# Hybrid encoder block on one core: full-row score and decay matmuls, and a quarter of the bias row copies

## The chip, the cores and the metric

The kernel runs on one core of a Trainium2 chip. The metric is the device time of one execution in microseconds, taken as the median of several runs.

## What is computed

One layer of a bidirectional encoder: 1024 tokens of width 1024. The normalised input goes through one projection whose columns serve two groups of heads: eight attention heads (two key heads, width 64) that see 128 tokens to either side, and four gated delta-rule heads (width 128) that run over the tokens in both directions. Their outputs pass `w_out`, and a feed-forward layer with a squared relu of width 4096 follows. The parts that matter here:

```
scores = einsum(q, k_band) * 64**-0.5 + bias[head, query, key - query]   # band: previous, own, next block of 128
scores = where(valid, scores, -1e30);  probs = softmax([scores, sink])
...
gc     = cumsum(g)                                     # per chunk, head, direction
decay  = exp(where(causal, gc[..., :, None] - gc[..., None, :], -inf))
a_mat  = where(strict, beta * (k @ k.T) * decay, 0);   t_mat = inverse(I + a_mat)
```

## The kernel before, in words

All large products are made in float32r with the operands split into a high and a low part: three matmuls of 128x512 for each 128 rows of the contraction (L118 to L122, `mm3`). Four engines work beside TensorE (PE): VectorE (DVE), ScalarE (ACT), GpSimd (POOL), and SyncE (SP), which issues nearly all the DMAs. PSUM is used as two rings of four banks, `psA` and `psB`; SBUF tiles come from rings too (`pg` with 28, `pt` with 12, `wr` with 4 buffers), so that a tile's buffer comes free when its last reader is done, a DMA included.

The program is written as Python generators that emit instructions, and `weave` (L51) runs two of them side by side by weights. A scheduler then sets the order on each engine once, at build time; each engine works through its own list in order. `phases` (L1026) has these stages:

- The input is normalised, transposed and split, and the a, b, k and q columns are projected. `gates` (L298) makes the cumulative decays `gc` by token and transposes them into rows; they are kept in three bfloat16 parts, two on the 128 rows of `g12`, the third on the 64 rows of `g3`.
- `bias_rows` (L500) makes the bias by relative position for 8 heads (8 x 512) with one matmul and writes it to DRAM, `biasd`, in 128 copies, one for each query row, so that reading with a pitch of 511 gives a band shifted by one per row.
- Projections of v, z and the attention's k, v, q are woven with `prep` (L615). For each of 8 chunks of 128 tokens and 2 directions, `prep` broadcasts a row of `gc` over all partitions for each of 4 heads: a matmul of a one-hot column (`selb`) against `g12` (L630), one of 64 rows against `g3` (L632), and one that adds the mask (L634). ScalarE takes the exponential (L637), VectorE multiplies by the Gram products (L641, L649), ScalarE copies the diagonal 32x32 blocks out (L646), and SP stores the results (`atd`, `pd`). Then `eliminate` (L653) inverts these blocks by 31 steps of elimination on VectorE for each direction (L669, L671; transposes L658, L680, L681), and `invert` (L685) builds the full inverses with small matmuls on PE (from L714).
- `proj_attn` (L457) keeps the attention keys' high part of each key head on both partition halves (`kh`, two tiles), and the low parts of both heads in one tile (`kl`), 64 rows each. Queries go to DRAM (`qad`, L493) and come back with the high part on 64 partitions and the low part on the other 64. `bias_table` (L514) loads the band of each pair of heads from `biasd` (L520).
- `attention` (L588) is woven with the first scan of the delta rule (`scan`, L762). For each block, key head and query head one matmul of 128 rows (L536: query high and low against key high) and one of 64 rows (L537: query high against key low) accumulate into a bank; VectorE adds the bias and takes the maximum (L538); exponentials on ScalarE (L550), scaling (L555), transposes on PE (L565), values (L576).
- The second scan runs beside the output projections, and then comes the feed-forward layer.

Of the kernel before, what the change touches and what calls it, by code (L numbers as in the profile page):

```python
# [9 lines left out]
F32 = mybir.dt.float32  # L10
# [23 lines left out]
def bucket_onehot():  # L34
    """Rows of the Toeplitz bias by relative position: 32 bucket selectors and the window mask."""
# [38 lines left out]
class Block:  # L74
# [30 lines left out]
    def small(self, shape, bufs=12, tag="sm"):  # L105
        return self.buf(tag, bufs, shape)
# [5 lines left out]
    def split(self, raw, h, l):  # L112
        """raw = h + l exactly, both float32r."""
# [34 lines left out]
    def setup2(self):  # L148
# [18 lines left out]
        self.selb = t("selb", (P, 64), BF16)  # L167
        nc.gpsimd.tensor_tensor(out=self.selb, in0=self.ident[:, 0:64], in1=self.ident[:, 64:128], op=ALU.add)
# [44 lines left out]
    def transpose_split(self, rows, w, pstag, out):  # L213
        """rows: 4 tiles [tok, D] -> per k a tile [d, (high, low), 512 tokens], scaled by w[:, k]."""
# [7 lines left out]
    def transpose_first(self, rows, w, out):  # L222
        """The same, row by row as the rows arrive, through all banks."""
# [8 lines left out]
    def load_w(self, srcs):  # L232
        """srcs(k half) -> list of (column slice, dram AP [p, 4, cols])."""
# [23 lines left out]
    def pair(self, raws, order=None):  # L257
        """The two column tiles of a load: (tile, half, psum), both tiles of one half first."""
# [39 lines left out]
    def gates(self, ps):  # L298
        """Per token: gc, its exponentials, beta. Layout [tok, chunk, dir * 4 + head]."""
# [35 lines left out]
        gc2 = self.small((P, 2, NT, 8), bufs=1, tag="gc2")  # L335
        self.ngc, self.egc, self.negc, self.egl, self.ew = (mk(n) for n in ("ngc", "egc", "negc", "egl", "ew"))
        for r in range(2):
            vt.tensor_copy(out=gc2[:, r], in_=gps[:, 0])
        vt.tensor_scalar(out=self.ngc, in0=gc2[:, 0], scalar1=-1.0, scalar2=None, op0=ALU.mult)
        nc.scalar.activation(out=self.egc, in_=gc2[:, 0], func=AF.Exp)  # L340
        vt.tensor_scalar(out=self.negc, in0=self.egc, scalar1=-1.0, scalar2=None, op0=ALU.mult)
        nc.scalar.activation(out=self.egl, in_=gps[:, 1], func=AF.Exp)
        vt.tensor_tensor(out=self.ew, in0=gps[:, 1], in1=gc2[:, 0], op=ALU.subtract)
        nc.scalar.activation(out=self.ew, in_=self.ew, func=AF.Exp)
        # gc by rows, in three bfloat16 parts
        tp = self.ps("psB", (P, P))
        nc.tensor.transpose(tp, gc2.rearrange("p r c x -> p (r c x)"), self.ident)
        self.g12 = c.tile([P, P], BF16, name="g12")
        self.g3 = c.tile([64, P], BF16, name="g3")
        rr = self.sc((P, 4, P))  # L350
        r1, b1 = rr[:, 0, :], rr[:, 1, :]
        nc.scalar.copy(out=self.g12, in_=tp)
        vt.tensor_copy(out=b1, in_=self.g12)
        vt.tensor_tensor(out=r1, in0=tp, in1=b1, op=ALU.subtract)
        vt.tensor_copy(out=self.g12[64:128, :], in_=r1[64:128, :])
        b2b = rr[0:64, 2, :]
        b2h = c.tile([64, P], BF16, name="b2h")
        vt.tensor_copy(out=b2h, in_=r1[0:64, :])
        vt.tensor_copy(out=b2b, in_=b2h)
        vt.tensor_tensor(out=self.g3, in0=r1[0:64, :], in1=b2b, op=ALU.subtract)  # L360
        self.cc, self.w2 = mk("cc"), mk("w2")

    def conv_silu(self, ct, raw, out):
        """Five taps along tokens, then silu."""
# [10 lines left out]
    def proj_conv(self, c0, kind, raws=None):  # L375
        """k, v or q columns of the delta rule heads, two heads a load."""
# [80 lines left out]
    def proj_attn(self):  # L457
        """Keys: the high part of each kv head on both partition halves, the low parts of both. Values: by tokens.
        Queries: scaled, to DRAM."""
# [4 lines left out]
        self.kh, self.kl = [self.pg(dt=F32R) for _ in range(2)], self.pg(dt=F32R)  # L464
        self.va = self.pg((P, NT, P))
        for i, half, ps in self.pair(raws):
# [3 lines left out]
            if i == 0:  # L470
# [3 lines left out]
                for v, (r, o) in enumerate(((lo, up), (up, lo))):  # L474
                    nc.scalar.copy(out=self.kh[v][r, tok], in_=t[r, :])
                    nc.scalar.copy(out=self.kh[v][o, tok], in_=swap[o, :])
                    nc.gpsimd.tensor_tensor(out=self.kl[r, tok], in0=t[r, :], in1=self.kh[v][r, tok].bitcast(F32),
# [22 lines left out]
    def bias_rows(self):  # L500
        """rel_bias by relative position, a copy per query row, so that rows of pitch 511 read it as a band."""
# [10 lines left out]
        nc.sync.dma_start(out=self.biasd, in_=row.unsqueeze(1).to_broadcast([8, P, 512]))  # L512

    def bias_table(self):  # L514
        self.bias = []
        for b in range(4):
            t = self.pg((P, 2, 3 * P))
            src = bass.AP(tensor=self.biasd.tensor, offset=self.biasd.offset + 2 * b * P * 512 + P - 1,
                          ap=[[511, P], [P * 512, 2], [1, 3 * P]])
            self.nc.sync.dma_start(out=t, in_=src)  # L520
            self.bias.append(t)

    def attn_scores(self, n, kv, mx, q, mk):
# [3 lines left out]
        rows = slice(64 * kv, 64 * kv + 64)  # L527
        tiles = []
        for gp in range(2):
            s = mk((P, 2, 3 * P))  # L530
            for i in range(2):
# [5 lines left out]
                nc.tensor.matmul(ps[:, :width], q[rows, g, :], self.kl[rows, keys], start=False, stop=True)  # L537
# [44 lines left out]
    def query(self, n, kv):  # L582
        """Queries' high parts on the partitions of their keys, the low parts on the others."""
# [4 lines left out]
    def attention(self):  # L588
        """Scores run ahead of the transposes of the probabilities by two steps of one block and key head."""
# [528 lines left out]
```

## Time and profile before

| | us |
|---|---|
| median of 3 runs (lowest, highest) | 1373.59 (1372.97, 1377.02) |
| span of the profiled execution | 1372.6 |
| PE busy in the span | 1335.4 |
| VectorE busy in the span | 661.1 |
| ScalarE busy in the span | 471.4 |
| windowed attention beside the first scan (358 to 515) | 157 |

The profile is of one execution. A row of a timeline gives the start, the length, the engine, the line in the kernel, the operation, and the tiles written and read. A matmul's length includes its way through the array, so that neighbours overlap: what a matmul costs in a row of others is read from start to start. Two engines can each be busy for most of a stage, and the stage ends with the one whose list ends last.

### The profile page before, as it was taken

The page shows a single profiled execution, that of the slowest core. Times are in us where ns is not written, and L with a number is a line of the kernel's source. Part 1 is how long each engine was busy: PE and PEld are TensorE (multiplying, and loading weights), DVE is VectorE, ACT ScalarE, POOL GpSimd, SP SyncE. Part 2 cuts the span into 40 slices and gives each one's busy share as a digit, 9 for nine tenths or more (in the row PEclk, how much of TensorE's full clock was granted, in tenths as well). Part 3 has the DMA queues.
Part 4 walks back from the last instruction along what each step waited for, and adds up shares of the span by engine and source line. Part 5 has one row for each costly group of instructions (what it writes and reads, how often), then busy time and mean ns, then how long its engine had stood idle before and what let it go on. Part 6 is the DMA issues. An engine that isn't in the chain of part 4 may idle for free.

```text
span 1372.6 us, 18620 instructions
## 1 busy us (share of the span) xinstructions
PE 1335.4 (97%) x7026; PEld 1056.2 (77%) x7026; DVE 661.1 (48%) x1339; ACT 471.4 (34%) x1085; POOL 463.3 (34%) x429
## 2 busy tenths in 40 slices
PE   7999969989999999999999999999999999999997
PEld 5788757868766668888888888888888888888885
DVE  4676636982467877575332233223332233223336
ACT  6464747445545553124412212122112211221113
POOL 4353200362422224143414332333323331433123
PEclk9999989999789999999999999999999999999999
DMA  6142463433835548121111110121011101121003
GB/s 218 62 135 97 65 196 124 146 116 80 214 108 147 161 153 305 64 62 62 62 32 62 62 47 16 62 62 62 16 46 62 62 31 32 62 62 57 20 1 123
DMA packets 86186, 121.97 MB, mean 89 GB/s; under 512 B 6627, under 2 KB 59952, under 8 KB 86097
## 3 DMA queue, kind: packets, MB, share of 16 engines
q1 hardware_dynamic: 77396, 116.30, 26.8%
q0 software_dynamic: 8448, 4.20, 1.6%
q8 instruction: 55, 0.90, 0.3%
q10 hardware_dynamic: 253, 0.30, 0.1%
q14 instruction: 34, 0.28, 0.1%
HBM read 88.79 MB, written 31.46 MB: 88 GB/s over the span
## 4 chain that ended last, share of the span: by engine, by line
PE 88%; DVE 6%; DMA 4%; issue 1%; ACT 1%; POOL 0%; POOLq 0%; DVEq 0%; ACTq 0%
PE psA L120 15%; PE psA L122 15%; PE psA L121 15%; PE psB L121 9%; PE psB L120 9%; PE psB L122 9%; PE psB L791 4%; DMA biasd<-pt 3%; PE psA L576 2%; PE psA L537 2%; PE psA L565 2%; DVE pt L669 2%; PE psA L536 2%; DVE sc L671 1%; DVE pg L671 1%
## 5 line engine op out<-in xcount | busy, mean ns | idle before, releaser
L122 PE MATMUL psA<-pg,wl 128*128 128x512 f32 x864 | 342.1, 397 | 0.8 <-POOL wl L116 0.8
L121 PE MATMUL psA<-pg,wh 128*128 128x512 f32 x864 | 342.3, 397 | 0.0
L120 PE MATMUL psA<-pg,wh 128*128 128x512 f32 x864 | 342.1, 397 | 0.2 <-ACT pg L208 0.2
L982 DVE TENSOR_TENSOR pg<-pg,psB 128x512 f32<-128x512 f32 x256 | 175.7, 688 | 277.1 <-PE psB L122 275.7
L116 POOL TENSOR_TENSOR wl<-wr,wh 128x512 fp32r<-128x512 f32 x108 | 156.3, 1469 | 291.6 <-ACT wh L115 291.5
L121 PE MATMUL psB<-sc,pg 128*128 128x512 f32 x512 | 202.5, 396 | 0.0
L120 PE MATMUL psB<-sc,pg 128*128 128x512 f32 x512 | 201.2, 394 | 0.0
L122 PE MATMUL psB<-sc,pg 128*128 128x512 f32 x512 | 200.8, 392 | 0.0
L122 PEld LDWEIGHTS psA<-pg,wl 128*128 128x128 f32 x864 | 163.0, 189 | 38.6 <-POOL wl L116 1.2
L121 PEld LDWEIGHTS psA<-pg,wh 128*128 128x128 f32 x864 | 163.0, 189 | 38.3 <-issue 0.9
L120 PEld LDWEIGHTS psA<-pg,wh 128*128 128x128 f32 x864 | 163.0, 189 | 37.8 <-ACT pg L208 0.6
L116 POOL TENSOR_TENSOR sc<-wr,sc 128x512 fp32r<-128x512 f32 x64 | 81.7, 1299 | 174.9 <-ACT sc L115 174.9
L964 DVE SCALAR_TENSOR_TENSOR pt<-psA,pt 128x512 f32<-128x512 f32 x64 | 44.1, 690 | 197.6 <-ACT pt L963 197.6
L966 POOL TENSOR_TENSOR pg<-pt,pg 128x512 fp32r<-128x512 f32 x64 | 82.2, 1294 | 157.4 <-ACT pg L965 157.4
L115 ACT CAST wh<-wr 128x512 fp32r<-128x512 f32 x108 | 61.7, 620 | 167.8 <-PE psA L121 144.4
L120 PEld LDWEIGHTS psB<-sc,pg 128*128 128x128 f32 x512 | 96.1, 188 | 23.9 <-ACT sc L115 0.6
L121 PEld LDWEIGHTS psB<-sc,pg 128*128 128x128 f32 x512 | 96.2, 188 | 22.6 <-POOL sc L116 0.5
L122 PEld LDWEIGHTS psB<-sc,pg 128*128 128x128 f32 x512 | 96.0, 188 | 22.3
L115 ACT CAST sc<-wr 128x512 fp32r<-128x512 f32 x64 | 36.4, 618 | 185.1 <-PE psB L121 185.1
L965 ACT CAST pg<-pt 128x512 fp32r<-128x512 f32 x64 | 39.6, 618 | 147.4 <-issue 122.3
L963 ACT ACTIVATE pt<-psA 128x512 f32<-128x512 f32 x64 | 37.8, 593 | 81.1 <-PE psA L122 81.1
L791 PE MATMUL psB<-sc,pg 128*128 128x128 f32 x320 | 47.8, 281 | 2.2 <-DVE pg L830 1.4
(288 smaller groups left out, 1774.2 us busy)
## 6 DMA issues: line engine op xcount, KB each, us to landing
wr<-in_w_ffn_in SPq DMA_DIRECT2D x32, 512.0 KB, 4.6
wr<-in_w_ffn_out SPq DMA_DIRECT2D x32, 512.0 KB, 3.6
wr<-in_w_in SPq DMA_DIRECT2D x22, 512.0 KB, 5.8
pg<-in_x SPq DMA_DIRECT2D x16, 512.0 KB, 5.2
sc<-kvd SPq DMA_DIRECT2D x14, 512.0 KB, 4.0
kvd<-pt SPq DMA_DIRECT2D x16, 256.0 KB, 4.4
atd<-pt SPq DMA_DIRECT2D x16, 256.0 KB, 5.0
pd<-pt SPq DMA_DIRECT2D x16, 256.0 KB, 3.3
```

What stands on the lines that cost most here:

```text
L115: nc.scalar.copy(out=h, in_=raw)
L116: nc.gpsimd.tensor_tensor(out=l, in0=raw, in1=h.bitcast(F32), op=ALU.subtract)
L120: nc.tensor.matmul(ps, wh, xh, start=first, stop=False)
L121: nc.tensor.matmul(ps, wh, xl, start=False, stop=False)
L122: nc.tensor.matmul(ps, wl, xh, start=False, stop=last)
L536: nc.tensor.matmul(ps[:, :width], q[:, g, :], self.kh[kv][:, keys], start=True, stop=False)
L791: nc.tensor.matmul(ps[:, h - g.start, :], left(h), right[:, h, :], start=True, stop=True)
L963: nc.scalar.activation(out=r, in_=ps, func=AF.Relu)
L964: nc.vector.scalar_tensor_tensor(out=q, in0=ps, scalar=0.0, in1=r, op0=ALU.max, op1=ALU.mult)
L965: nc.scalar.copy(out=a[:, 0], in_=q)
L966: nc.gpsimd.tensor_tensor(out=a[:, 1], in0=q, in1=a[:, 0].bitcast(F32), op=ALU.subtract)
L982: nc.vector.tensor_tensor(out=self.h[t][:, sl], in0=self.h[t][:, sl], in1=ps, op=ALU.add)
```

## The change

- `prep`: the three parts of the decay rows are laid on rows 0 to 47 of one tile `grow` (row 16 r + 2 chunk + direction for part r, the four heads side by side on the free axis), with zeros on the other rows. `selb` has ones at i, i + 16 and i + 32. One matmul of 128 rows and 512 columns makes the rows of all four heads, and one of 512 columns adds the mask.
- `gates`: one copy of `gc` where there were two; the parts are made on 64 rows, written to DRAM (`gcd`, three DMAs), and read back as `grow` (one DMA).
- `proj_attn` and `attn_scores`: a tile of low key parts for each key head, with zeros on the 64 rows that held the other head, so that the second score matmul has 128 rows as well. VectorE writes the zeros.
- `bias_rows` and `bias_table`: 32 copies of each bias row, not 128; the table of two heads is loaded by four DMAs of 32 partitions, each from another offset.

The diff, cut to its core:

```diff
-        self.selb = t("selb", (P, 64), BF16)
-        nc.gpsimd.tensor_tensor(out=self.selb, in0=self.ident[:, 0:64], in1=self.ident[:, 64:128], op=ALU.add)
+        self.selb, self.zero = t("selb", (P, 16), BF16), t("zero", (P, 1))
+        nc.gpsimd.memset(self.zero, 0.0)
+        nc.gpsimd.tensor_tensor(out=self.selb, in0=self.ident[:, 0:16], in1=self.ident[:, 16:32], op=ALU.add)
+        nc.gpsimd.tensor_tensor(out=self.selb, in0=self.selb, in1=self.ident[:, 32:48], op=ALU.add)
...
+        self.grow = c.tile([P, GH, P], BF16, name="grow")
+        nc.gpsimd.memset(self.grow, 0.0)
+        for r in range(3):
+            nc.sync.dma_start(out=self.gcd[r], in_=part[:, r, :])
+        nc.sync.dma_start(out=self.grow[0:48], in_=self.gcd.rearrange("r (a h) t -> (r a) h t", h=GH))
...
-        self.kh, self.kl = [self.pg(dt=F32R) for _ in range(2)], self.pg(dt=F32R)
+        self.kh, self.kl = [self.pg(dt=F32R) for _ in range(2)], [self.pg(dt=F32R) for _ in range(2)]
+        for v, o in enumerate((up, lo)):
+            nc.vector.tensor_copy(out=self.kl[v][o, :], in_=self.zero[o, :].to_broadcast([64, SEQ]))
...
-        nc.sync.dma_start(out=self.biasd, in_=row.unsqueeze(1).to_broadcast([8, P, 512]))
+        nc.sync.dma_start(out=self.biasd, in_=row.unsqueeze(1).to_broadcast([8, 32, 512]))
...
-            src = bass.AP(tensor=self.biasd.tensor, offset=self.biasd.offset + 2 * b * P * 512 + P - 1,
-                          ap=[[511, P], [P * 512, 2], [1, 3 * P]])
-            self.nc.sync.dma_start(out=t, in_=src)
+            for m in range(4):
+                src = bass.AP(tensor=self.biasd.tensor,
+                              offset=self.biasd.offset + 2 * b * 32 * 512 + P - 1 - 32 * m,
+                              ap=[[511, 32], [32 * 512, 2], [1, 3 * P]])
+                self.nc.sync.dma_start(out=t[32 * m:32 * m + 32], in_=src)
...
-                nc.tensor.matmul(ps[:, :width], q[rows, g, :], self.kl[rows, keys], start=False, stop=True)
+                nc.tensor.matmul(ps[:, :width], q[:, g, :], self.kl[kv][:, keys], start=False, stop=True)
...
-                for h in range(GH):
-                    i = 8 * c + 4 * d + h
-                    nc.tensor.matmul(rows[:, h, :], self.selb[:, i:i + 1].to_broadcast([P, P]), self.g12,
-                                     start=True, stop=False)
-                    nc.tensor.matmul(rows[:, h, :], self.selb[0:64, i:i + 1].to_broadcast([64, P]), self.g3,
-                                     start=False, stop=False)
-                    nc.tensor.matmul(rows[:, h, :], self.identb, self.maskb[d], start=False, stop=True)
+                i = 2 * c + d
+                nc.tensor.matmul(rows, self.selb[:, i:i + 1].to_broadcast([P, P]), self.grow, start=True, stop=False)
+                nc.tensor.matmul(rows, self.identb, self.maskb[d].unsqueeze(1).to_broadcast([P, GH, P]),
+                                 start=False, stop=True)
```

The scheduler sets the order anew, and it differs at many places by a few rows. Three of them follow; line numbers after the change are those of the changed file, which runs two to three lines ahead at these places.

PE's list at the first chunk's decay rows, before (`g_507` is `g12`, `g_508` is `g3`, and the three matmuls with their loads follow for each head):

```order
L630 LDWEIGHTS selb
L630 MATMUL psB_1292<-g_507,selb 128x128
L632 LDWEIGHTS selb
L632 MATMUL psB_1292<-g_508,selb 128x128
L634 LDWEIGHTS identb
L634 MATMUL psB_1292<-maskb_127,identb 128x128
```

The same place after the change, with the first matmul of the chunk's second direction behind it (`psB_1318`):

```order
L633 LDWEIGHTS selb
L633 MATMUL psB_1298<-grow,selb 128x512
L634 LDWEIGHTS identb
L634 MATMUL psB_1298<-maskb_128,identb 128x512
L633 LDWEIGHTS selb
L633 MATMUL psB_1318<-grow,selb 128x512
```

What stood there were 12 matmuls for each direction, and now there are 2. The projection matmuls among which they stand moved too: ahead of the last decay row of all there are 664 `mm3` matmuls in PE's list, where there were 636; ahead of the first matmul of the inversion 870, where there were 879; ahead of the first score 1056 in both.

VectorE's list near the end of the elimination, before (`pg` tiles are of the first direction, `sc` tiles of the second, L469 empties a bank of the key projection):

```order
L671 TENSOR_TENSOR pg_2075<-pg_2075,pt_2078 128x31
L669 TENSOR_TENSOR pt_2388<-sc_2383,sc_2385 128x220
L680 STREAM_TRANSPOSE pg_2342<-pg_2075 128x1024
L681 STREAM_TRANSPOSE pg_2341<-pg_2075 128x1024
L671 TENSOR_TENSOR sc_2385<-sc_2385,pt_2388 128x10x22
L469 COPY pt_2616<-psA_2591 128x512
```

The same place after the change:

```order
L672 TENSOR_TENSOR pg_1921<-pg_1921,pt_1924 128x31
L672 TENSOR_TENSOR sc_2231<-sc_2231,pt_2234 128x6x26
L681 STREAM_TRANSPOSE pg_2188<-pg_1921 128x1024
L682 STREAM_TRANSPOSE pg_2187<-pg_1921 128x1024
L467 CAST pg_2375<-zero 64x1024
L467 CAST pg_2376<-zero 64x1024
L670 TENSOR_TENSOR pt_2234<-sc_2229,sc_2231 128x135
L484 COPY pg_2379<-psB_2467 128x512
```

The two fills of zeros stand between the end of the first direction's elimination and the end of the second's.

SP's list at the bias table, before (`atd` loads feed the inversion, `qad` stores are the queries):

```order
L493 DMA qad<-pt_3044 64x512 x2
L520 DMA pg_3315<-biasd 128x2x384
L520 DMA pg_3317<-biasd 128x2x384
L520 DMA pg_3319<-biasd 128x2x384
L520 DMA pg_3321<-biasd 128x2x384
L701 DMA pg_3360<-atd 128x2x512
L701 DMA pg_3364<-atd 128x2x512
```

The same place after the change:

```order
L496 DMA qad<-pt_2893 64x512 x2
L525 DMA pg_3164<-biasd 32x2x384 x4
L525 DMA pg_3169<-biasd 32x2x384 x4
L525 DMA pg_3174<-biasd 32x2x384 x4
L525 DMA pg_3179<-biasd 32x2x384 x2
L496 DMA qad<-pt_2968 64x512 x2
```

Sixteen loads stand where four stood; the last two of them, and the two `atd` loads of a later step, come behind further query stores.

More of the change, by code (lines that the diff above doesn't have):

```diff
@@ L103, in pt, with small @@
         return self.buf("pt", 12, shape, dt)
-    def small(self, shape, bufs=12, tag="sm"):
-        return self.buf(tag, bufs, shape)
+    def small(self, shape, bufs=12, tag="sm", dt=F32):
+        return self.buf(tag, bufs, shape, dt)
     def ps(self, tag, shape=(P, HALF)):
@@ L334, in gates @@
         nc.tensor.matmul(gps[:, 1], self.ones, g, start=True, stop=True)
-        gc2 = self.small((P, 2, NT, 8), bufs=1, tag="gc2")
+        gc2 = self.small((P, NT, 8), bufs=1, tag="gc2")
         self.ngc, self.egc, self.negc, self.egl, self.ew = (mk(n) for n in ("ngc", "egc", "negc", "egl", "ew"))
[L337 to L340, printed above, removed]
+        vt.tensor_copy(out=gc2, in_=gps[:, 0])
@@ L341, in gates @@
+        vt.tensor_scalar(out=self.ngc, in0=gc2, scalar1=-1.0, scalar2=None, op0=ALU.mult)
+        nc.scalar.activation(out=self.egc, in_=gc2, func=AF.Exp)
         vt.tensor_scalar(out=self.negc, in0=self.egc, scalar1=-1.0, scalar2=None, op0=ALU.mult)
         nc.scalar.activation(out=self.egl, in_=gps[:, 1], func=AF.Exp)
-        vt.tensor_tensor(out=self.ew, in0=gps[:, 1], in1=gc2[:, 0], op=ALU.subtract)
+        vt.tensor_tensor(out=self.ew, in0=gps[:, 1], in1=gc2, op=ALU.subtract)
         nc.scalar.activation(out=self.ew, in_=self.ew, func=AF.Exp)
-        tp = self.ps("psB", (P, P))
@@ L347, in gates @@
[L347 to L360, printed above, removed]
+        tp = self.ps("psB", (64, P))
+        nc.tensor.transpose(tp, gc2.rearrange("p c x -> p (c x)"), self.ident)
+        rr = self.sc((64, 2, P))
+        part = self.small((64, 3, P), bufs=1, tag="gparts", dt=BF16)
+        nc.scalar.copy(out=part[:, 0, :], in_=tp)
+        vt.tensor_copy(out=rr[:, 0, :], in_=part[:, 0, :])
@@ new lines, in gates @@
+        vt.tensor_tensor(out=rr[:, 1, :], in0=tp, in1=rr[:, 0, :], op=ALU.subtract)
+        vt.tensor_copy(out=part[:, 1, :], in_=rr[:, 1, :])
+        vt.tensor_copy(out=rr[:, 0, :], in_=part[:, 1, :])
+        vt.tensor_tensor(out=part[:, 2, :], in0=rr[:, 1, :], in1=rr[:, 0, :], op=ALU.subtract)
+        self.grow = c.tile([P, GH, P], BF16, name="grow")
[3 more added lines that the diff above has]
+        nc.sync.dma_start(out=self.grow[0:48], in_=self.gcd.rearrange("r (a h) t -> (r a) h t", h=GH))
@@ L476, in proj_attn @@
                     nc.scalar.copy(out=self.kh[v][o, tok], in_=swap[o, :])
-                    nc.gpsimd.tensor_tensor(out=self.kl[r, tok], in0=t[r, :], in1=self.kh[v][r, tok].bitcast(F32),
+                    nc.gpsimd.tensor_tensor(out=self.kl[v][r, tok], in0=t[r, :], in1=self.kh[v][r, tok].bitcast(F32),
                                             op=ALU.subtract)
@@ L526, in attn_scores @@
         width, boff = (hi - lo) * P, (lo - (n - 1)) * P
-        rows = slice(64 * kv, 64 * kv + 64)
         tiles = []
@@ L1017, in build @@
             d = lambda name, shape: dram.tile(list(shape), F32, name=name)
-            self.biasd = d("biasd", (8, P, 512))[:]
+            self.biasd = d("biasd", (8, 32, 512))[:]
+            self.gcd = dram.tile([3, 64, P], BF16, name="gcd")[:]
             self.zd, self.mad = d("zd", (GH, P, SEQ))[:], d("mad", (NT, P, HALF))[:]
```

## The prediction

> **What bounds the kernel now.** I read the page first: its span, its busy times and the chain that ended last.
>
> ```profile
> span 1372.6 us, 18620 instructions
> PE 1335.4 (97%) x7026; PEld 1056.2 (77%) x7026; DVE 661.1 (48%) x1339; ACT 471.4 (34%) x1085; POOL 463.3 (34%) x429
> PE 88%; DVE 6%; DMA 4%; issue 1%; ACT 1%; POOL 0%; POOLq 0%; DVEq 0%; ACTq 0%
> ```
>
> TensorE is nearly always busy and carries 88% of the chain, so work taken from it counts, unless another engine is next in line at that place. Which one that is shows in windows cut at the stages that the change touches: decay rows and projections (142 to 250), the elimination (250 to 305), the inversion (305 to 358), windowed attention beside the first scan (358 to 515).
>
> ```profile
> 142.00:188.00 46.00, 36.70 (x222) 28.09 (x222) 21.95 (x39) 27.69 (x62) 7.08 (x8) 0.94 0.52 75
> 188.00:250.00 62.00, 60.66 (x354) 45.67 (x354) 39.69 (x80) 44.11 (x103) 9.59 (x10) 0.93 0.53 182
> 250.00:305.00 55.00, 51.03 (x220) 40.23 (x218) 53.94 (x129) 16.28 (x28) 30.54 (x17) 1.00 0.38 120
> 305.00:358.00 53.00, 52.93 (x620) 43.20 (x621) 13.48 (x26) 27.23 (x45) 17.31 (x19) 1.00 0.49 137
> 358.00:515.00 157.00, 157.00 (x1162) 103.65 (x1162) 116.71 (x377) 86.19 (x239) 43.30 (x43) 0.91 0.51 145
> ```
>
> The columns are length, then busy PE, PEld, DVE, ACT and POOL, the granted clock, and DMA. PE has a hole of 9 us in the first row. The third row is VectorE's (53.94 of 55). The others are PE's. The longest waits of 140 to 305 name the hole's cause, and SP's timeline and the chain in order of time show the transfer behind it.
>
> ```profile
> DVE pt L641 <- DMA biasd<-pt: 13.8, 1, 13.8
> PE psB L630 <- DVE pt L641: 10.6, 1, 10.6
> ```
>
> ```profile
> 142.08 0.81 SPq L512 DMA_DIRECT2D biasd<-pt  x1
> 146.84 23.19 SPq L238 DMA_DIRECT2D wr<-in_w_in  x2
> ```
>
> ```profile
> 142.08 45.40 DMA biasd<-pt
> ```
>
> The bias rows take 45.4 us to write. They hold a `pt` buffer that VectorE needs for the decay products, and SP's next two loads need 23 us to be issued. TensorE waits 10.6 us for it all.
>
> **The bias rows: a quarter of the copies.** The same 2 KB rows, 256 instead of 1024, take 45.4 / 4 = 11.4 us by that row, so the buffer is free at 153.5. The wait goes: -10.6. Behind it the clock was down, as windows of 10 us show.
>
> ```profile
> 190.00:200.00 10.00, 10.00 (x45) 6.63 (x44) 3.54 (x11) 7.85 (x22) 0.12 (x1) 0.68 0.87 327
> 200.00:210.00 10.00, 10.00 (x68) 7.65 (x67) 9.15 (x15) 4.81 (x14) 2.39 (x2) 1.00 0.61 187
> 370.00:380.00 10.00, 10.00 (x50) 6.92 (x49) 5.92 (x26) 6.94 (x20) 3.15 (x4) 0.50 0.20 46
> ```
>
> Ten us at 0.68 hold 6.8 us of work, and at 200 the clock is back: -3.2. (The third row is used further down.)
>
> **The decay rows.** The PE timeline of one direction of one chunk (the first two rows are ordinary projection matmuls; first column the start):
>
> ```profile
> 150.16 0.39 PE L120 MATMUL psA<-pg,wh 128*128 128x512 f32 x1
> 150.39 0.40 PE L121 MATMUL psA<-pg,wh 128*128 128x512 f32 x1
> ...
> 156.38 0.23 PE L630 MATMUL psB<-g,selb 128*128 128x128 bf16 x1
> 156.54 0.23 PE L632 MATMUL psB<-g,selb 64*128 64x128 bf16 x1
> 156.70 0.23 PE L634 MATMUL psB<-maskb,identb 128*128 128x128 bf16 x1
> 156.76 0.22 PE L630 MATMUL psB<-g,selb 128*128 128x128 bf16 x1
> ...
> 157.87 0.47 PE L121 MATMUL psA<-pg,wh 128*128 128x512 f32 x1
> ```
>
> Into and out of the 64-row matmul it is 0.16 us from start to start, between two 128-row ones 0.06. Twelve matmuls take 157.87 - 156.38 = 1.49 us. Two of 512 columns take 2 x 0.23 = 0.46 by the first two rows (1.03 saved), 16 times: -16.5. The replanned order puts 28 more projection matmuls ahead of the last decay row (664 against 636, at 0.23): +6.4. So that row moves by -10.6 - 3.2 - 16.5 + 6.4 = -23.9. ScalarE stands close behind: 71.8 us busy from 142 to 250 (27.69 + 44.11), which must now fit into some 84. Some of that comes back; between nothing and 8 us I take 4. The elimination starts 20 us earlier.
>
> **Elimination and the zeroed low keys.** VectorE fills this stage, from the transposed diagonal blocks to the first inversion matmul that reads the last result:
>
> ```profile
> 242.82 1.25 DVE L658 STREAM_TRANSPOSE pg<-pg 128x1024 f32<-128x1024 f32 x1 [0.67 <-ACT pg L646]
> ```
>
> ```profile
> 305.07 0.22 PE L714 MATMUL psB<-sc,pg 32*32 32x32 f32 x1 [0.43 <-DVE sc L681]
> ```
>
> The change adds two fills of 64x1024 to VectorE, and the order shows them inside the second direction's elimination. The nearest row is a 128x1024 pass:
>
> ```profile
> L368 DVE TENSOR_SCALAR pg<-sc,cols 128x1024 f32<-128x1024 f32 x8 | 7.5, 950 | 13.6 <-ACT sc L389 13.6
> ```
>
> I take 1.1 us each with the neighbour POOL active (0.9 to 1.4), and 1 us for a key tile that VectorE must await earlier than before: +3.2. TensorE can't use its gain here. Its queue has 425 projection matmuls (434 before) between the bias rows' matmul, just ahead of the write at 142, and the first inversion matmul: 425 x 0.23 = 98, decay rows 16 x 0.46 = 7.4, and 18 for 64 Gram products of two passes and 36 transposes (164 passes at the 0.11 of the 128-column rows further down). That ends at 265, and then it waits for VectorE until 305 - 20 + 3.2 = 288. So PE gets a hole of some 20 us where it had 4 (51.03 of 55). Price of the clock after it, by the hole of 10.6 above: +3.2; nine matmuls that now stand behind it: +2.1. Up to the first score: -20 + 3.2 + 3.2 + 2.1 = -11.5.
>
> [...]
>
> **The scores.** PE rows of two heads, 384 and then 256 keys wide, of heads in the slow zone, and eight 128-row matmuls with as many weight loads:
>
> ```profile
> 398.62 0.44 PE L536 MATMUL psA<-pg,pt 128*128 128x384 f32 x1
> 398.99 0.44 PE L537 MATMUL psA<-pg,pt 64*128 64x384 f32 x1
> 399.36 0.45 PE L536 MATMUL psA<-pg,pt 128*128 128x384 f32 x1
> ```
>
> ```profile
> 362.11 0.38 PE L536 MATMUL psA<-pg,pt 128*128 128x256 f32 x1
> 362.42 0.38 PE L537 MATMUL psA<-pg,pt 64*128 64x256 f32 x1
> 362.73 0.38 PE L536 MATMUL psA<-pg,pt 128*128 128x256 f32 x1
> ```
>
> ```profile
> 366.41 0.69 PE L536 MATMUL psA<-pg,pt 128*128 128x384 f32 x1
> 367.03 0.69 PE L537 MATMUL psA<-pg,pt 64*128 64x384 f32 x1
> ```
>
> ```profile
> 533.24 1.05 PE L791 MATMUL psB<-sc,sc 128*128 128x128 f32 x8
> 534.13 0.61 PE L791 MATMUL psB<-sc,pg 128*128 128x128 f32 x4
> ```
>
> A pair takes 0.74 us at 384 keys and 0.62 at 256, of which the columns explain 0.175 and 0.12 a matmul (at 0.23 per 512). A weight load costs no more than 0.11 (0.89 / 8). So a pair should take 0.35 or 0.24: 48 x 0.39 + 16 x 0.38 = 24.8 us less PE. The zeros add no column. Does PE's gain become time? VectorE is busy 116.7 of these 157 us, and would have to do it in 132; each scan step goes to it and back, and each score waits for one of four banks that it empties. Bounds: 5 (VectorE sets the pace) to 24.8; I take 65%, -16, since PE is busy in all of the 157 us now and VectorE in three quarters. Part of this stage has the clock at 0.5 (row 370:380); the mean of 0.91 over 157 us makes 14 us of lost clock. Denser matmuls may shorten that: -4, of 0 to -14.
>
> **The bias table** comes in 16 loads, not 4, and SP's order has most of them ahead of 24 query stores.
>
> ```profile
> L520 SPq DMA_DIRECT2D pg<-biasd x4: 359/363/367, 338.4 to 341.3; - x4
> ```
>
> ```profile
> 343.36 20.22 SPq L493 DMA_DIRECT2D qad<-pt  x24
> ```
>
> Twelve more issues of 0.36 are 4.3 us of SP, behind which the query stores wait; TensorE still has projections then: +1, of 0 to 4.3.
>
> [...]
>
> **Edits with one answer.** The decay parts go through DRAM and back over SP, where the key stores are queued behind the read's wait:
>
> ```profile
> kvd<-pt SPq DMA_DIRECT2D x16, 256.0 KB, 4.4
> ```
>
> That wait is bounded by one landing, 4.4 us, some 60 us ahead of the first reader, with projections in between: nothing. POOL's fills stand at the very start, where it waits for the first squares:
>
> ```profile
> 6.30 0.19 POOL L184 TENSOR_SCALAR sm<-sm 128x1 f32<-128x1 f32 x1 [2.50 <-ACT pt L197]
> ```
>
> Two and a half us of idle time take them: nothing. Without that cover they would cost under 1 us each.
>
> **Sum.** -11.5 - 16 - 4 + 1 = -30.5. The profiled span, 1372.6, becomes 1342; the median of the runs is 1 us above that span: 1343.
>
> **Rivals.** *Everything arrives*: ScalarE takes nothing back (-4), the hole costs no clock (-3.2), scores give 24.8 and the slow zone two thirds of its 14: -18.7 - 24.8 - 9 = -52.5, 1321. For it: PE is the one busy engine from 358 to 515. Chance 0.17. *VectorE takes over in attention*: -11.5 - 5 = -16.5, 1357; for it its 75% share there. Chance 0.20. *The row count is not what the matmuls wait for*, but each new weight load: the scores stay; -11.5, 1362. Against it: 0.06 between 128-row loads. Chance 0.06. *The bias loads stand in the path*: SP is held as in the 23 us row and the first score waits; 12 x 0.84 (as the query stores, 20.22 us for 24) = 10 us back, 1353. [...] Against it: the table is issued by 341.3, the scores begin at 358. Chance 0.06. *Slower*: the hole of 20 us and the small inversion matmuls hold the clock at 0.5 through the whole inversion, as around 370. Its 186 projection matmuls then take 43 us more, with the 3.2 in it: -30.5 + 40 = +9.5, 1383; it decides from about 31 us of dense matmuls at half clock. Against it: after the hole of 10.6 us the clock was full again from 200 on. Chance 0.05. The forecast has 0.46.
>
> **Range and chances.** 1319 to 1363 holds all but the slow rival and the far side of the first. A difference under 0.3% (4 us) can't be told from none. All but the slow rival are faster; a hundredth of it falls within the bound: 0.94, 0.01, 0.05.
>
> **What would show it.** Right: the wait for `biasd` gone; 2 matmuls of 512 bf16 columns in 0.5 us; a PE hole of 10 to 25 us ending at 280 to 295 on VectorE's last transpose; score pairs at 0.35 us; PE waiting for VectorE in attention. Wrong: pairs still at 0.7, no hole (then ScalarE or the order held PE), or a clock below 0.7 over more than 40 us after 285.

## The result, and the profile after

The changed kernel takes 1328.74 us (median of 4 runs, 1328.16 to 1330.21), the kernel before 1373.7 beside it: 0.9665 of it, 95% interval 0.9646 to 0.9684; that is 45 us less by the medians, 46 by the ratio. Forecast were 1343, within 1319 to 1363.

The head of the page after:

```profile
span 1326.6 us, 18332 instructions
PE 1291.2 (97%) x6866; PEld 1041.0 (78%) x6866; DVE 649.7 (49%) x1339; ACT 469.8 (35%) x1085; POOL 460.9 (35%) x432
```

The windows of its stages (length; busy PE, PEld, DVE, ACT and POOL; granted clock; DMA share and GB/s; PEld is the loading of weights into TensorE):

```profile
142.00:216.00 74.00, 73.64 (x392) 59.72 (x391) 52.19 (x96) 62.19 (x143) 15.58 (x14) 1.00 0.48 150
216.00:281.60 65.60, 59.45 (x255) 46.72 (x254) 57.93 (x151) 25.99 (x51) 29.95 (x23) 0.95 0.43 137
281.60:338.00 56.40, 53.13 (x610) 43.69 (x611) 13.38 (x25) 23.42 (x40) 17.11 (x18) 0.94 0.44 110
338.00:456.10 118.10, 113.60 (x1076) 86.88 (x1075) 100.34 (x347) 78.27 (x219) 35.90 (x37) 0.97 0.64 174
```

The span is 46.0 us shorter and PE is busy 44.2 us less; the other engines do nearly what they did. The first row has no hole left in PE; the gain is spread over the stages, and the last row is the largest piece. To see where time went, follow four marks through both traces: the last decay row, VectorE's last transpose of the elimination, the first and the last score. The view of one line gives them (shortest, median and longest in ns, then first and last start in us). Before:

```profile
L634 PE MATMUL psB<-maskb,identb x64: 229/229/289, 146.7 to 239.8; 128*128 128x128 bf16 x64
L681 DVE STREAM_TRANSPOSE sc<-sc x1: 2033/2033/2033, 303.0 to 303.0; 128x1024 f32<-128x1024 f32 x1
L536 PE MATMUL psA<-pg,pt x64: 280/438/689, 358.3 to 500.6; 128*128 128x384 f32 x48, 128*128 128x256 f32 x16
```

After:

```profile
L634 PE MATMUL psB<-maskb,identb x16: 379/379/379, 146.3 to 215.4; 128*128 128x512 bf16 x16
L682 DVE STREAM_TRANSPOSE sc<-sc x1: 1878/1878/1878, 279.7 to 279.7; 128x1024 f32<-128x1024 f32 x1
L540 PE MATMUL psA<-pg,pt x64: 281/417/606, 338.0 to 456.1; 128*128 128x384 f32 x48, 128*128 128x256 f32 x16
```

So the marks (last decay row, last transpose, first and last score) move by -24.4, -23.3, -20.3 and -44.5. Nearly all of the gain is made before attention ends.

TensorE's waits from 140 to 520, after (who waited for what, total, times, longest, in us):

```profile
PE psB L756 <- ACT pt L750: 3.3, 1, 3.3
PE psA L120 <- ACT pt L454: 2.1, 1, 2.1
PE psB L405 <- DVE pt L650: 1.7, 1, 1.7
PE psB L715 <- DVE sc L682: 1.6, 1, 1.6
...
PE psA L540 <- DMA pt<-qad: 0.4, 1, 0.4
```

The 10.6 us behind the bias write are gone. The hole of some 20 us before the inversion that was forecast is a wait of 1.6.

### The profile page after: what moved, and what is told of

Its sections match the earlier page's. It is cut to its first block, busy times and chain, and to the rows that moved or that the text cites. A ratio compares the mean times of both kernels' runs of the same rounds, so it can differ in the third digit from the quotient of the medians.

```text
span 1326.6 us, 18332 instructions
## 1 busy us (share of the span) xinstructions
PE 1291.2 (97%) x6866; PEld 1041.0 (78%) x6866; DVE 649.7 (49%) x1339; ACT 469.8 (35%) x1085; POOL 460.9 (35%) x432
## 4 chain that ended last, share of the span: by engine, by line
PE 71%; DVE 1%; DMA 0%; issue 0%; ACT 0%; POOLq 0%; POOL 0%; SPq 0%; DVEq 0%; ACTq 0%
PE psA L120 11%; PE psA L121 11%; PE psA L122 11%; PE psB L121 9%; PE psB L120 9%; PE psB L122 9%; PE psB L792 4%; PE psA L580 2%; PE psA L569 1%; PE psA L540 1%; PE psA L541 1%; PE psB L205 0%; DMA pg<-in_w_out 0%; PE psB L756 0%; PE psA L905 0%
## 5 line engine op out<-in xcount | busy, mean ns | idle before, releaser
L116 POOL TENSOR_TENSOR wl<-wr,wh 128x512 fp32r<-128x512 f32 x108 | 152.7, 1435 | 282.4 <-ACT wh L115 282.2
L116 POOL TENSOR_TENSOR sc<-wr,sc 128x512 fp32r<-128x512 f32 x64 | 81.7, 1300 | 174.9 <-ACT sc L115 174.9
L120 PEld LDWEIGHTS psB<-sc,pg 128*128 128x128 f32 x512 | 96.1, 188 | 23.9 <-ACT sc L115 0.6
```

The lines of the kernel that those rows point to most:

```text
L116: nc.gpsimd.tensor_tensor(out=l, in0=raw, in1=h.bitcast(F32), op=ALU.subtract)
L120: nc.tensor.matmul(ps, wh, xh, start=first, stop=False)
```

## The experiments

Each kernel ran beside the kernel before on the same chip. Ratios are to that kernel; "clock lost" is the sum over windows of 10 us from 320 to 520 of 10 x (1 - granted clock). Ratios rest on all runs of a kernel; marks and clock lost are of one profiled run each, and two such runs of the changed kernel differ by 3.2 us at the last score and 3.4 in clock lost.

| kernel | ratio (95% interval) | last decay row | last transpose | first score | last score | clock lost |
|---|---|---|---|---|---|---|
| before | 1 | 239.8 | 303.0 | 358.3 | 500.6 | 13.7 |
| changed | 0.9665 (0.9646 to 0.9684) | 215.4 | 279.7 | 338.0 | 456.1 | 6.8 |
| before + bias part | 0.9904 (0.9887 to 0.9922) | 226.9 | 290.1 | 346.0 | 489.5 | 11.9 |
| before + decay rows | 0.9904 (0.9888 to 0.9920) | 229.9 | 290.4 | 345.1 | 489.9 | 17.1 |
| before + scores | 0.9781 (0.9766 to 0.9796) | 239.9 | 302.9 | 358.4 | 474.8 | 1.7 |
| before, bias row in its own tile | 0.9956 (0.9941 to 0.9971) | 235.0 | 298.5 | 354.5 | 501.1 | 18.8 |
| before, 64-row matmul twice | 1.0126 (1.0107 to 1.0145) | 240.2 | 303.4 | 359.4 | 518.0 | 20.5 |
| changed, bias part undone | 0.9771 (0.9751 to 0.9791) | 230.6 | 295.3 | 351.6 | 473.8 | 8.5 |
| changed, 64-row scores | 0.9839 (0.9823 to 0.9855) | 216.2 | 279.7 | 340.3 | 482.5 | 15.3 |
| changed, eight decay matmuls | 0.9653 (0.9639 to 0.9667) | 212.5 | 277.4 | 331.7 | 453.6 | 8.5 |
| the same again | 0.9633 (0.9612 to 0.9654) | 212.6 | 277.5 | 331.9 | 454.0 | 8.5 |
| changed, fills five times | 0.9701 (0.9686 to 0.9716) | 215.6 | 285.3 | 336.1 | 463.3 | 10.2 |
| changed, fills on ScalarE | 0.9693 (0.9679 to 0.9708) | 215.6 | 277.7 | 331.8 | 460.3 | 13.6 |
| changed, again | 0.9664 (0.9644 to 0.9683) | 215.5 | 279.8 | 338.1 | 459.3 | 10.2 |

### One part at a time

**The bias part alone.**

```diff
-        nc.sync.dma_start(out=self.biasd, in_=row.unsqueeze(1).to_broadcast([8, P, 512]))
+        nc.sync.dma_start(out=self.biasd, in_=row.unsqueeze(1).to_broadcast([8, 32, 512]))
...
+            for m in range(4):
+                self.nc.sync.dma_start(out=t[32 * m:32 * m + 32], in_=src)
```

> The kernel before with the bias part alone (32 copies of each bias row, the table of two heads in four loads). Theory: the wait of VectorE for the pt buffer and TensorE's 10.6 us behind it go, and so do the 3.2 us of low clock behind them; the last decay row is 11 to 14 us earlier, the elimination and the first score follow in full, and the time falls by 11 to 14 us. Rival 1, the gain ends on ScalarE or VectorE ahead of the elimination: under 5 us. Rival 2, the sixteen table loads stand in the path: first score held at L540's place, gain under 4 us.

1363.86 against 1377.19: -13.2 by the ratio. The last decay row comes 12.9 us earlier, and the low clock behind the wait is gone (in the 34 us from 170 on it is 0.9 or more by the page's slice, where the kernel before has 0.80); the first score follows by 12.3. The theory holds; the gain ends on neither ScalarE nor the loads ahead of attention.

**The decay rows alone.**

```diff
-                for h in range(GH):
-                    i = 8 * c + 4 * d + h
...
+                i = 2 * c + d
+                nc.tensor.matmul(rows, self.selb[:, i:i + 1].to_broadcast([P, P]), self.grow, start=True, stop=False)
+                nc.tensor.matmul(rows, self.identb, self.maskb[d].unsqueeze(1).to_broadcast([P, GH, P]),
+                                 start=False, stop=True)
```

> The kernel before with the decay rows alone (two matmuls of 128 rows and 512 columns for twelve, the rows gathered through DRAM). The wait for the bias write stays and ends at 188 whatever the decay rows cost. Theory: the rows that come before that wait save nothing, some 12 to 14 of 16 lie behind it and save 1.03 us each, so the last decay row is 12 to 15 us earlier and the time falls by 12 to 15 us. Rival, the ScalarE exponentials pace this stretch: under 6 us.

1363.24: -13.2. The last decay row comes 9.9 us earlier, less than expected here; TensorE waits 12.4 us for the bias write, not 10.6, since it gets there sooner. The first score is 13.2 earlier, more than the decay rows explain: VectorE's elimination, from its first transpose to its last, is shorter too, 55.8 us (234.6 to 290.4) in place of 60.2 (242.8 to 303.0), and the cause of that stays open.

**The scores alone.**

```diff
+        for v, o in enumerate((up, lo)):
+            nc.vector.tensor_copy(out=self.kl[v][o, :], in_=self.zero[o, :].to_broadcast([64, SEQ]))
...
-                nc.tensor.matmul(ps[:, :width], q[rows, g, :], self.kl[rows, keys], start=False, stop=True)
+                nc.tensor.matmul(ps[:, :width], q[:, g, :], self.kl[kv][:, keys], start=False, stop=True)
```

> The kernel before with the scores alone (low keys of each key head on a tile of 128 rows, half of it zeros). Theory: what the pairs cost is the change of row count between neighbours, so they go from 0.74 to 0.35 us (384 keys) and from 0.62 to 0.24 (256); that is 24.8 us less TensorE and nearly all of it becomes time, since in the changed kernel attention was 24 us shorter; the fills cost up to 2: the time falls by 20 to 25 us. Rival 1, VectorE paces attention and the changed kernel's gain there came from the earlier stages and their clock: 5 to 12 us. Rival 2, each new weight load is the price: pairs unchanged, no gain.

1347.12: -30.2 by the ratio, more than any theory had. Nothing moves before the first score, and from there to the last score it takes 116.4 us, not 142.3. Beside the fills the pairs were all that was changed, but their own length is not the whole size: the clock lost falls from 13.7 to 1.7 us as well. Windows of 10 us, this kernel:

```profile
370.00:380.00 10.00, 8.27 (x105) 5.85 (x107) 8.04 (x31) 9.80 (x27) 4.13 (x4) 1.00 0.36 100
380.00:390.00 10.00, 10.00 (x196) 7.19 (x186) 9.69 (x29) 6.24 (x15) 3.52 (x5) 1.00 0.55 143
```

The kernel before has 0.50 in 370 to 380, the row that the prediction quotes.

The three parts add up to -56.6 by their ratios, where the whole gives -46. By the marks of the single profiles the last scores add up to -47.6 (11.1, 10.7 and 25.8), where the whole has -44.5. The clock explains as much as the marks differ: the parts save 1.8 and 12.0 us of clock and lose 3.4, 10.4 together, and the whole saves 6.9. That the ratios differ by more is not settled.

### One part undone

**The bias part undone in the changed kernel** (128 copies, four loads: the first diff read backwards).

> The changed kernel with the bias part undone (128 copies of each row, the table in four loads). Theory, the parts add up: the wait for the write comes back at 187, the last decay row moves from 215 to 226 to 230, and the time rises by 9 to 13 us against the changed kernel. Rival, the other two parts now hide it, or the sixteen loads cost what the copies save: under 4 us.

1346.0 beside 1330.45 for the changed kernel on that chip: 15.5 us, or 14.7 by the ratios, a little over the range. The wait is back at 12.4 us, and the last decay row at 230.6.

**The second score matmul on 64 rows** (the changed kernel, its tiles and fills kept).

```diff
-                nc.tensor.matmul(ps[:, :width], q[:, g, :], self.kl[kv][:, keys], start=False, stop=True)
+                nc.tensor.matmul(ps[:, :width], q[rows, g, :], self.kl[kv][rows, keys], start=False, stop=True)
```

> The changed kernel with one edit: the second score matmul reads only the 64 rows that are not zeros (same tiles, same fills, same number of matmuls, same result). Theory, the change of row count is the price: pairs at 0.74 and 0.62 us again, attention 20 to 25 us longer, 1349 to 1354 us. Rival, the gain in attention came from another source (layout, order, clock): pairs at 0.35, time within 4 us of the changed kernel's 1328.7.

1355.12, 24 us more than the changed kernel by the ratios; attention takes 142.2 us again. Layout, fills and number of matmuls are unchanged, so the row count makes the difference here. One of its pairs in the PE timeline:

```profile
412.63 0.44 PE L541 MATMUL psA<-pg,pt 128*128 128x384 f32 x1
413.00 0.43 PE L542 MATMUL psA<-pg,pt 64*128 64x384 f32 x1
```

Its windows in the first part of attention:

```profile
350.00:360.00 10.00, 10.00 (x119) 6.84 (x107) 6.37 (x27) 8.73 (x25) 3.50 (x4) 0.50 0.39 99
360.00:370.00 10.00, 10.00 (x31) 5.70 (x32) 5.05 (x19) 4.69 (x14) 1.34 (x1) 0.58 0.10 20
```

The two of a pair are 0.37 from start to start again, and the clock is at 0.50 and 0.58 with them.

### Is it the change of rows, or the 64 rows?

**The 64-row matmul twice** (kernel before).

```diff
                 nc.tensor.matmul(ps[:, :width], q[:, g, :], self.kh[kv][:, keys], start=True, stop=False)
+                nc.tensor.matmul(ps[:, :width], q[rows, g, :], self.kl[rows, keys], start=False, stop=False)
                 nc.tensor.matmul(ps[:, :width], q[rows, g, :], self.kl[rows, keys], start=False, stop=True)
```

> The kernel before, with the 64-row score matmul issued twice in a row for each head (the low part is counted twice, so the output is not the reference's). 64 matmuls are added, nearly all right behind their twin, so the number of changes between 64 and 128 rows stays as it is. Theory, the price lies in the change of row count: the second of the two starts 0.17 us (384 keys) or 0.12 (256) after the first, 64 x 0.16 = 10 us more TensorE, and the time rises by 6 to 11 us. Rival, a 64-row matmul is slow by itself: 0.37 and 0.31 us from start to start, 64 x 0.36 = 23 us more, and the time rises by 18 to 23 us.

1392.39 against 1373.95: +18.4 by the medians and +17.3 by the ratio, at the lower edge of the rival's range and above the theory's, so the time alone speaks for the rival. The rows tell which it is. The PE timeline (L537 and L538 are the twins):

```profile
396.14 0.44 PE L536 MATMUL psA<-pg,pt 128*128 128x384 f32 x1
396.51 0.44 PE L537 MATMUL psA<-pg,pt 64*128 64x384 f32 x1
396.79 0.33 PE L538 MATMUL psA<-pg,pt 64*128 64x384 f32 x1
397.05 0.44 PE L536 MATMUL psA<-pg,pt 128*128 128x384 f32 x1
```

Three matmuls take 397.05 - 396.14 = 0.91 us, the pair before took 0.74: the twin adds 0.17, which is what a 128-row one adds. Two changes cost 0.74 - 0.35 = 0.39 us. The weight loads of the same stretch (PEld) show what a change costs:

```profile
396.51 0.18 PEld L537 LDWEIGHTS psA<-pg,pt 64*128 64x128 f32 x1 [0.19 <-issue]
396.62 0.19 PEld L538 LDWEIGHTS psA<-pg,pt 64*128 64x128 f32 x1
397.05 0.19 PEld L536 LDWEIGHTS psA<-pg,pt 128*128 128x128 f32 x1 [0.25 <-issue]
```

The twin's load starts at 396.62, 0.17 ahead of its matmul and beside the matmul before it. The loads behind a change of row count start only with their own matmul (396.51, 397.05), and nothing hides them. A load of 0.19 and the 0.175 of 384 columns make the 0.37 from start to start; so do loads of 0.10, by the same view of the kernel before, and 0.06 the 0.16 of the bfloat16 decay rows. In the kernel before all 64 loads of L537 start within 0.002 us of their matmul; in the changed kernel 63 of the 64 of L541 start 0.11 us or more ahead. So the price lies in the change of row count, as the theory had it, and here it is as long as a weight load that no longer runs ahead: 0.195 us a change beside loads of 0.18 to 0.19. What the theory missed is the clock: some 10 us more TensorE and 6.8 us more of clock lost (20.5 against 13.7) make the 17.

**Eight decay matmuls of 128 columns for two of 512** (changed kernel), in two runs.

```diff
-                nc.tensor.matmul(rows, self.selb[:, i:i + 1].to_broadcast([P, P]), self.grow, start=True, stop=False)
-                nc.tensor.matmul(rows, self.identb, self.maskb[d].unsqueeze(1).to_broadcast([P, GH, P]),
-                                 start=False, stop=True)
+                for h in range(GH):
+                    nc.tensor.matmul(rows[:, h, :], self.selb[:, i:i + 1].to_broadcast([P, P]), self.grow[:, h, :],
+                                     start=True, stop=False)
+                    nc.tensor.matmul(rows[:, h, :], self.identb, self.maskb[d], start=False, stop=True)
```

> The changed kernel with the decay rows made head by head: for each direction of a chunk four matmuls of 128 columns from the gathered rows and four for the mask, eight with eight weight loads in place of two with two; all have 128 rows. Theory, twelve matmuls cost 1.49 us because of the changes of row count: eight of 128 rows take 8 x 0.06 = 0.48 us, as the two do (0.46), and the time stays within 3 us of the changed kernel. Rival, the number of matmuls and weight loads was the price: 8/12 of 1.49 = 1.0 us, 16 x 0.54 = 8.6 us of TensorE more, and the time rises by 6 to 9 us.

> The changed kernel with eight decay matmuls of 128 columns for two of 512, again, beside the changed kernel on one chip. If the first bank quarter being ready earlier lets ScalarE start earlier, the elimination starts 2 us earlier and the time is 1 to 2 us below the changed kernel's; if the earlier difference was one of chips, they are the same within 1 us.

1326.86, then 1325.72 beside 1330.45: 1.6 and 4.3 us less by the ratios, with intervals that overlap. Four times as many matmuls and loads cost nothing that the rows show, and all have 128 rows. PE timeline of the second profile:

```profile
154.83 0.23 PE L634 MATMUL psB<-grow,selb 128*128 128x128 bf16 x1
154.89 0.22 PE L636 MATMUL psB<-maskb,identb 128*128 128x128 bf16 x1
...
155.26 0.47 PE L120 MATMUL psA<-pg,wh 128*128 128x512 f32 x1
```

155.26 - 154.83 = 0.43 us for eight, against 1.49 for twelve of mixed rows. The few us less need not be theirs: the planner put 649 projection matmuls, not 664, ahead of the last decay row, and 15 x 0.23 = 3.45 us is about the 2.9 by which that row is earlier. It has the lowest ratio here, by what looks like an accident of the order.

### How the bias write hurts

**The bias row in a tile of its own** (kernel before; all engines keep their order).

```diff
-        row = self.pt((8, 512))
+        row = self.const.tile([8, 512], F32, name="brow")
```

> The kernel before, with the bias row in a tile of its own, not in a buffer of the pt ring; still 128 copies of each row and a write of some 45 us. Every engine has the order of before. Theory as the prediction has it, the write hurts through the buffer that it holds: VectorE's wait of 13.8 us for it goes, TensorE's 10.6 us with it, and the time falls by 10 to 13 us, as with a quarter of the copies. Rival, the write hurts through the queue: SP's loads of 23 us and the decay stores of 14 us behind it are issued as late as before, and TensorE or VectorE waits for what they bring or free at nearly the same point; the time falls by 0 to 4 us.

1369.99 against 1377.38: -6.1 by the ratio, between the two. (The profiled run, 1374.17, lies above that median: its last score is no earlier than before, with 5.1 us more of clock lost.) VectorE's wait for the row's buffer is gone; it now waits for ScalarE's exponentials, and ScalarE for a buffer. ScalarE's timeline:

```profile
191.68 2.39 ACT L637 ACTIVATE pt<-psB,ngc 128x128 f32<-128x128 f32 x8 [13.38 <-DMA atd<-pt]
```

SP's timeline:

```profile
146.76 23.16 SPq L238 DMA_DIRECT2D wr<-in_w_in  x2
170.03 14.22 SPq L648 DMA_DIRECT2D atd<-pt  x2
```

TensorE's longest wait:

```profile
PE psB L404 <- ACT pt L637: 6.3, 1, 6.3
```

SP needs as long as before for what stands behind the write (23.19 us for the loads and 14.18 for the stores in the kernel before). The decay products' stores (`atd`) are 14 us in being issued, and they hold the next buffers of the ring, for which ScalarE waits 13.4 us. TensorE waits 6.3 in place of 10.6. So both readings were true, one behind the other, and of the kernels here only the one with the shorter write is rid of both: in the changed kernel the same loads take 5.14 us and the stores 1.90, by SP's timeline:

```profile
146.53 5.14 SPq L240 DMA_DIRECT2D wr<-in_w_in  x2
151.77 1.90 SPq L649 DMA_DIRECT2D atd<-pt  x2
```

### What sets the start of attention

**The fills five times over** (changed kernel).

```diff
+            for _ in range(5):
-            nc.vector.tensor_copy(out=self.kl[v][o, :], in_=self.zero[o, :].to_broadcast([64, SEQ]))
+                nc.vector.tensor_copy(out=self.kl[v][o, :], in_=self.zero[o, :].to_broadcast([64, SEQ]))
```

> The changed kernel with each of the two fills of zeros written five times (same values, so the result is the same): eight more passes of 0.7 to 1.6 us on VectorE, 6 to 11 us, inside the second direction's elimination. The planner's order then has 46 projection matmuls, not 26, between the first inversion matmul and the one that reads the second direction. Theory 1, VectorE sets the end of this stage and what it loses is lost: the first score and the end are 5 to 9 us later. Theory 2, TensorE covers it: 20 more matmuls x 0.23 = 4.6 us are put into the gap, which only moves work, so the loss is what is left, 2 to 5 us. Theory 3, the gap opens and the clock pays too: 9 to 13 us.

1332.8: 4.9 us more than the changed kernel by the ratios, on the border of theories 1 and 2. The marks part them: VectorE's last transpose is 5.6 later, TensorE waits 2.5 for it, not 1.6, and the first score is not later but 1.9 earlier. The cover is as theory 2 has it. What was lost came later, at a place that no theory named:

```profile
PE psA L541 <- DMA pt<-qad: 8.1, 1, 8.1
PE psB L716 <- DVE sc L683: 2.5, 1, 2.5
```

The scores that follow wait 8.1 us for their queries. In the timelines of SP and POOL the last four bias loads stand behind 11 us of query stores, and POOL's next query load waits for them:

```profile
324.55 11.00 SPq L497 DMA_DIRECT2D qad<-pt  x16
335.64 1.94 SPq L526 DMA_DIRECT2D pg<-biasd  x4
...
337.91 0.79 POOL L590 DMA_DIRECT2D pt<-qad  x1 [8.81 <-DMA pg<-biasd]
```

**The fills on ScalarE** (changed kernel).

```diff
-            nc.vector.tensor_copy(out=self.kl[v][o, :], in_=self.zero[o, :].to_broadcast([64, SEQ]))
+            nc.scalar.copy(out=self.kl[v][o, :], in_=self.zero[o, :].to_broadcast([64, SEQ]))
```

> The changed kernel with the two fills of zeros written by ScalarE, not VectorE. Theory, VectorE sets the end of the elimination: without the 2.3 us of fills its last transpose, and with it the inversion, comes 1 to 2.3 us earlier; the time falls by 0 to 2.5 us. Rival, the fills are covered by the projection matmuls: within 1 us of the changed kernel, or slower by the 2 us that ScalarE is late with something that TensorE waits for.

1332.99, 3.8 us slower by the ratios, whose intervals overlap at the edge. The transpose comes 2.0 earlier, as expected, and the first score 6.2 earlier; then TensorE waits 4.6 us for the queries, the clock lost doubles to 13.6, and the last score is 4.2 later. Being early at attention is worth little while the queries are late: with the eight decay matmuls too TensorE waits 4.9 us for them, and of 6.3 us at the first score 2.5 are left at the last. The bias loads need not be the cause. With the bias part undone there are four of them, and POOL's query load still waits 8.83 us (for a query store) and TensorE 4.0. No run put the query stores, or the bias loads, on another queue.

**The changed kernel again.**

> The changed kernel once more, as the mark on this chip for the next kernel: 0.9665 of the kernel before, within 0.002.

1330.45, 0.9664. Its profiled span is 1329.8, 3.2 us over that of the first profile, and its clock lost is 10.2 against 6.8: the same program, with 3.4 us more of clock lost.

## Why the prediction came out right, and which steps did not

**Bias, decay rows and order: right, to a microsecond.** Forecast were -13.8 for the bias part (measured alone: -12.9), -16.5 + 6.4 = -10.1 for the decay rows with the new order (-9.9), -23.9 together (-24.4). For the decay rows alone the hit is partly luck, since TensorE waited 1.8 us longer for the bias write there. The mechanism behind the first was only half told: the buffer is the first of two things that the write holds.

**ScalarE takes back 4 us: too much.** 1.7 was lost on the way to the elimination, which starts at 220.1 in place of 242.82, -22.7.

```profile
L659 DVE STREAM_TRANSPOSE pg<-pg x1: 1246/1246/1246, 220.1 to 220.1; 128x1024 f32<-128x1024 f32 x1
```

**Elimination +3.2: wrong sign.** The fills are there (2.33 us for the two, forecast 2.2), and with ScalarE doing them the last transpose is 2.0 earlier. The first ran beside a pass of POOL (L116, 266.71 to 269.27) and took 1.63 us, the second beside none and took 0.69. Yet the stage, 59.6 us from 220.1 to the last transpose at 279.7, is not longer than before (60.2): VectorE's row shows no wait ahead of the fills, where 1 us was taken. Without the fills it would be shorter still, as in the kernel with the decay rows alone (55.8); the cause is open, as said there. The row of the two fills:

```profile
268.19 2.33 DVE L467 CAST pg<-zero 64x1024 fp32r<-64x1024 f32 x2
```

**"So PE gets a hole of some 20 us": failed.** The forecast hole from 265 to 288 is one of 1.6 us in the PE timeline, so the prediction's own sign of being wrong, no hole, came true:

```profile
273.14 0.39 PE L122 MATMUL psA<-pg,wl 128*128 128x512 f32 x1
273.45 0.28 PE L715 MATMUL psB<-pg,pg 32*32 32x32 f32 x2
273.66 0.50 PE L120 MATMUL psA<-pg,wh 128*128 128x512 f32 x1
...
279.58 0.39 PE L121 MATMUL psA<-pg,wh 128*128 128x512 f32 x1
281.59 0.22 PE L715 MATMUL psB<-sc,pg 32*32 32x32 f32 x1 [1.61 <-DVE sc L682]
```

The window in which TensorE lost time on its way there:

```profile
220.00:230.00 10.00, 6.17 (x21) 4.56 (x20) 8.66 (x22) 6.11 (x12) 3.60 (x5) 0.66 0.81 275
```

Three errors add up. The queue was counted to the first inversion matmul, but the one that reads the second direction stands 26 projection matmuls further on (896 against 870; before the change it was 6), 6 us of cover. TensorE reaches the first one at 273.45, not 265, because it had small waits (2.1 and 1.7 above) and a low clock behind the last decay row, at 220 to 230; 3.8 us of idle time and some 2 of clock in that window make most of it. And VectorE was done 6.4 us sooner than forecast. The planner puts projection matmuls into such a gap: 46 with five times the fills.

**Clock price +3.2 behind the hole, and nine matmuls +2.1: too much by 2, and by other causes.** The nine were counted from the first inversion matmul too. Behind the one that reads the second direction stand 160 projection matmuls, 11 fewer than before (171), not nine more. From the first inversion matmul on the second direction to the first score it took 53.2 us before (305.07 to 358.3) and now 56.4 (+3.2), with a wait of 3.3 for ScalarE and the clock at 0.66 in 320 to 330:

```profile
320.00:330.00 10.00, 7.71 (x46) 6.71 (x47) 3.86 (x6) 4.36 (x8) 4.97 (x4) 0.66 0.83 195
```

Because of these steps the first score was forecast 11.5 us earlier and came 20.3 earlier. That is the larger part of the 14 us by which the forecast was off.

**Score pairs at 0.35 and 0.24: right in a run of pairs, not between other work.** After:

```profile
391.98 0.44 PE L540 MATMUL psA<-pg,pt 128*128 128x384 f32 x1
392.26 0.34 PE L541 MATMUL psA<-pg,pt 128*128 128x384 f32 x1
392.44 0.60 PE L792 MATMUL psB<-sc,sc 128*128 128x128 f32 x4
...
396.97 0.33 PE L540 MATMUL psA<-pg,pt 128*128 128x384 f32 x1
397.14 0.34 PE L541 MATMUL psA<-pg,pt 128*128 128x384 f32 x1
397.32 0.34 PE L540 MATMUL psA<-pg,pt 128*128 128x384 f32 x1
```

In a run 397.32 - 396.97 = 0.35, by itself between values and scan 392.44 - 391.98 = 0.46. There the first matmul takes 0.28: it stands behind a values matmul of 128 rows and 64 columns (form 128*64), and its load of 0.19 us too starts with it, at 391.98 by the PEld timeline, not ahead. Summed over the recorded pairs, from the first start to the next matmul, 64 pairs took 49.6 us before, and the 63 that stand together after took 28.2; by the forecast's prices it would be 45.4 and 20.6. That the price lies in the change of row count is shown by the twin and its loads above: 0.39 us for a change there and back.

**65% of it becomes time, and the clock gives 4: the first right, the second too low.** Busy time by mean clock is taken as work at full clock: projection matmuls start 0.43 us apart at a granted 0.50 (before, 194 to 196), and 0.23 at 1.00 (198 to 200). Before:

```profile
358.30:500.60 142.30, 142.30 (x1076) 94.55 (x1074) 105.61 (x347) 77.36 (x218) 37.26 (x39) 0.90 0.51 141
```

142.3 x 0.90 = 128.1 of work, against 113.60 x 0.97 = 110.2 after: 17.9 us less, where 16 were forecast. Clock lost while busy falls from 14.2 to 3.4, 10.8 us, where 4 (of 0 to 14) were taken. PE idles 4.5 us more. Sum -24.2, against -19 with the bias loads. VectorE did not take over: it is busy 100.34 of 118.1 us, and the longest wait of a score for it is 0.8 us.

**Bias loads +1: about right here.** TensorE waits 0.4 us for queries. In three kernels that reach attention sooner it waits 4.6 to 8.1, but with the bias part undone, later and with four loads, it waits 4.0, so the rival is not shown by that.

**The rivals.** "New weight loads are the price" fell as it was put, to the twin and the eight decay matmuls: the pairs got shorter with as many loads. But what a change of row count costs here is as long as a load (0.19 us), one that doesn't run ahead. "VectorE takes over" fell to the row above. "Half clock through the inversion" did not come: the clock is 0.94 in 281.6 to 338. "Everything arrives" was nearest at the first score and for the clock in attention, and too hopeful for the scores.

## What to carry to other kernels

Read what a small matmul costs from start to start, and look at the row counts (first number of the form) of its neighbours: here filling up to 128 rows took 2.33 us of VectorE, once, and a pair in a run went from 0.74 to 0.35 us, with 64 pairs in all. Then look whether each weight load starts ahead of its matmul (after, 63 of the 64 of L541) or with it (before, all 64 of L537). When a long transfer holds a buffer, look at what stands behind it on its queue too, since freeing the buffer alone gave about half of the gain here (-6.1 of -13.2 us). And before forecasting a hole, count the queue up to the instruction that reads the late result, not to the first of its kind.

## What was unexpected of the hardware

The granted clock stays at 0.50 for 20 us while the rows show TensorE busy 10.00 of 10 (before, 370 to 390; the window of 10 us ahead of it is as busy, at 0.68), in the part of attention where 64-row scores stand among 32x32 inversion matmuls. The five kernels with 64-row pairs lost 11.9 to 18.8 us of clock from 320 to 520, 20.5 with the twin, and the kernel before with only the scores changed lost 1.7. So busy rows alone did not keep the clock up here; what lowers it no run here tells. Row counts are not all of it: kernels with 128-row pairs lost up to 13.6, and that one (fills on ScalarE) waited 4.6 us for queries as well. Whether the pauses at each change of rows, where a weight load runs by itself, lower the clock was not tried by itself.
